# Modulation vectors of one layer computed beside another stage of a two-block model

## The chip, the cores and the metric

The kernel runs on 1 core of one Trainium2 chip. The metric is the device time of one execution in microseconds (us). PE is TensorE (the matrix engine), PEld its loads of stationary operands, DVE VectorE, ACT ScalarE, POOL GpSimd, SP SyncE, whose queue issues nearly all DMAs here.

## What is computed

The reference runs two blocks on 1024 latent rows of 1024 features, with context rows of 256 beside them. The first block has one layer: a mixer (half of the width a Hyena long convolution, half a bidirectional HGRN scan with four heads, which starts from the context's state) and a mixture of 16 experts. The second block has two layers of another mixer (Fourier, pooling, differential attention over context and latent rows). In both, vectors that depend on the conditioning alone scale and shift the rows:

```python
# first block
sh1, sc1, g1, sh2, sc2, g2 = jnp.split((s_lat @ ada_w[l] + ada_b[l])[:, None, :], 6, axis=-1)
h = modulate(rmsnorm(x, norm1_g[l]), sh1, sc1)
x = x + g1 * mix
h2 = modulate(rmsnorm(x, norm2_g[l]), sh2, sc2)
x = x + g2 * ec_moe(h2, ...)
...
# second block, layer l
shift, scale, gate = jnp.split(jax.nn.silu(c) @ w_mod + b_mod, 3, axis=-1)
shift_c, scale_c, gate_c = jnp.split(jax.nn.silu(c_ctx) @ w_mod + b_mod, 3, axis=-1)
hc = rms_norm(ctx, norm_g) * (1 + scale_c) + shift_c
```

The second block's `w_mod` is 1024 x 3072 for each layer. These products hang on no row of the latent or the context, so they can be made at any time before their first use.

## The kernel before

`run` (L1993) writes the whole program in stages. Each opens pools of tiles (a tag with a number of buffers, on the left or the right of the memory), and a tile of a tag waits until one of the tag's buffers is free. The program's order is not the engines' order: a planner (`schedule_with_timeline_sim`) fills each engine's queue at build time. Of the instructions that it holds ready it takes the one written first, so work written later fills the places that earlier work leaves. On the chip each queue then runs strictly in the order made.

The stages around the change, with the tiles by which the trace names them:

- *Projection stage.* Three streams are written interleaved by `side_by_side` (L1979): the Hyena filter and convolution (`filter_time`, `filter_spectra`, `hyena`; products into `pf`, their operands made in `y`, `t`, `fb`, `f`), the projections of the latent rows (`hy_proj`, `hg_proj`; weights `ar`, split into `ah` and `al`, products into `pp`, with the rows in `T`), and `mods_layer(0, ...)`, the modulation vectors of the second block's layer 0. `ctx_proj` of the stage ahead still runs at its beginning (`pp<-c,cr`).
- *The heads' stage.* `ctx_state` and four calls of `hgrn_head` (L944), two heads at a time in pools of their own (`hi`, `hw`, `hm`, `hT`, products into `ph`). A head runs seven levels: copies on ScalarE, products on TensorE, a masked copy (L985) and products over `hw` and `hT` on VectorE and GpSimd. A tail with more products follows. The heads read what the projections wrote, and their pools lie where the projections' tiles lay.
- *The context's work* of the second block is written behind the heads and fills in beside them: `mods_tail` (the rest of the first block's vectors: `g1`, `sh2`, `sc2`, `g2`), `ctx_first` (context rows, normed and modulated with layer 0's vectors), `ctx_side` (two column blocks, then `gate_steps`; products into `cp` and `cm`), and `mods_layer(1, ...)`.
- *Output product* `out_proj` (L1095; `pp<-wo,yt`), which reads `g1` and, in its router, `sh2` and `sc2`; then `topk`, then the experts (`moe`, products into `ea` and `ey`).

The change moves one call of `mods_layer` (L333). It runs `mod_rows` (L290) with three blocks of 1024 columns, each of eight k-steps:

```python
        for b0 in range(c0, c0 + ncols, 1024):
            ps = self.ps(pt)
            for k in range(8):
                if not pair:
                    r = self.t(raw[k % len(raw)])
                    self.dma(r, w[k * 128:k * 128 + 128, b0:b0 + 1024])
...
                for cb in range(2):
                    p0 = 64 * (k % 2) + 32 * cb
                    self.mm(ps[p0:p0 + 2], s[:, k, :], r[:, cb * 512:cb * 512 + 512], k < 2, k > 5)
```

One k-step is called a unit below: a load of 512 KB and, in the trace, four products with a stationary operand of two columns. A block ends with two bias loads, four additions on VectorE and two writes to DRAM. After the third block `rows_to_cols` (L315) reads the rows back as columns (two loads, one transpose, one copy), and two small operations make `A`. In `mods_layer(0, "mp", "u2", ("mr",), False)` the units pass through one buffer `mr`; in `mods_tail("cm", "cv", ("wr", "wr", "mr"), False)` through two buffers `wr` and one `mr`. The context's weights (`wcol`, then `wh` and `wl`) use `wr` too.

Of the kernel before, what the change touches and what calls it, by code (L numbers as in the profile page):

```python
# [1992 lines left out]
def run(K):  # L1993
    fst = ExitStack()
    with ExitStack() as e1:
        K.open(e1, "left", ar=3, ah=4, al=4)
        K.open_ps(e1, "left", pp=3, mp=1)
        K.open(e1, "left", u2=4, T=16)
        K.open_ps(fst, "right", pf=4)
        K.open(fst, "right", f4=7, fb=5)  # L2000
        with ExitStack() as e2:
            K.open(e2, "right", cr=6, x=4, c=2, mr=4)
            K.start()
        K.open(fst, "right", y=3, t=4, H=2, hs=3, dc=2, ri=7, ra=2, mr=1)
        K.load_dft()
        K.mods_first()
        side_by_side((30, 450, [(K.filter_time(), 2.4), (K.filter_spectra(), 2.1), (K.hyena(), 5)]),
                   (0, 64, [(K.hy_proj(), 1), (K.hg_proj(), 1)]),
                   (0, 4, [(K.mods_layer(0, "mp", "u2", ("mr",), False), 1)]))
    fst.close()  # L2010
    with ExitStack() as cx:
        with ExitStack() as e1:
            K.open_ps(e1, "left", ph0=3, ph1=3)
            K.open(e1, "left", hmk=1, hS=2)
            for p in "01":
                K.open(e1, "left", **{"hi" + p: 6, "hw" + p: 5, "h2" + p: 3, "hm" + p: 4, "hT1" + p: 2, "hT2" + p: 4})
            K.ctx_state()
            for h in range(4):
                K.hgrn_head(h)
            K.open(cx, "right", wr=2, wh=2, wl=2, cu=6, cv=2, Tc=4, lg=2)  # L2020
            K.pfx = "c"
            with ExitStack() as e2:
                K.open_ps(e2, "right", cp=1, cm=1)
                K.open(e2, "right", mr=1)
                for _ in K.mods_tail("cm", "cv", ("wr", "wr", "mr"), False):
                    pass
                K.ctx_first()
                K.ctx_side()
                for _ in K.mods_layer(1, "cm", "cv", ("wr", "wr", "mr"), False):
                    pass  # L2030
# [27 lines left out]
class Kern:  # L2058
# [9 lines left out]
    def start(self):  # L2068
        W = self.work
        W.pc, W.psm, W.pd, W.one = self.pc, self.psm, self.pd, self.one  # L2070
        run(W)
# [119 lines left out]
```

## Time and profile before

| | us |
|---|---|
| median of 3 runs | 3840.05 |
| lowest, highest | 3839.73, 3846.28 |
| the profiled execution | 3841.8 |
| its span, first to last instruction | 3839.7 |

By the page, TensorE is busy 92% of the span, VectorE 71%, ScalarE 58%, GpSimd 29%. Its table of 40 slices (96 us each) shows a DMA share of 0.9 and more only in the experts' part. The views used below are: the table of stretches (busy time of each engine in a stretch, count of instructions in brackets, the granted clock of TensorE as a share of full speed, the DMA engines' share and GB/s), groups of instructions (line, engine, operation, out<-in, shapes, count, then busy us and mean ns, then the idle time before them and what ended it), instructions by tile (least, median and most ns, first and last start), and the instructions in order of time.

### The profile page before, as it was taken

What the parts mean: (1) busy time and instruction counts of PE and PEld (TensorE: products, weight loads), DVE (VectorE), ACT (ScalarE), POOL (GpSimd) and SP (SyncE); (2) the same over time, 40 slices, a digit from 0 to 9 for tenths busy, and PEclk for the clock granted to TensorE, in tenths of its full rate; (3) what the DMA queues carried; (4) which work ended last, traced back from release to release, by engine and by line L of the source; (5) the groups of instructions that cost most, each with busy time, mean ns of one, the idle gap of its engine ahead of it and who ended that gap; (6) DMA issues with size and microseconds to landing.
All of it is one profiled execution on the core that took longest, in us unless ns stands there. A gap on an engine that the chain in (4) does not pass through costs nothing. (4 is left out here: it accounts for less than half of the span.)

```text
span 3839.7 us, 50939 instructions
## 1 busy us (share of the span) xinstructions
PE 3533.6 (92%) x17554; PEld 2841.9 (74%) x17554; DVE 2727.8 (71%) x4143; ACT 2219.1 (58%) x3568; POOL 1127.8 (29%) x702
## 2 busy tenths in 40 slices
PE   5998999968897799999999999979999899999989
PEld 2666878747867678787777777768777688877767
DVE  3488667777735789889889889866666744576672
ACT  4432322354525786787777777755576754456762
POOL 2355423364414214112112111001333610133361
PEclk9999999979998899999999999989999999999999
DMA  6765444464476699999999999952311144131133
GB/s 206 220 222 181 130 145 128 141 211 147 132 246 218 200 341 347 336 333 364 371 366 358 370 367 357 364 185 81 128 60 43 47 155 132 59 128 54 39 104 115
DMA packets 503019, 780.49 MB, mean 203 GB/s; under 512 B 35025, under 2 KB 238823, under 8 KB 502504
## 3 DMA queue, kind: packets, MB, share of 16 engines
q1 hardware_dynamic: 496136, 755.74, 57.8%
q0 software_dynamic: 5600, 20.43, 2.0%
q8 instruction: 138, 2.26, 0.2%
q10 hardware_dynamic: 1024, 1.06, 0.1%
q14 instruction: 121, 0.99, 0.1%
HBM read 669.00 MB, written 107.05 MB: 202 GB/s over the span
## 5 line engine op out<-in xcount | busy, mean ns | idle before, releaser
L171 DVE TENSOR_TENSOR el<-er,eh 128x1024 fp32r<-128x1024 f32 x763 | 950.7, 1296 | 107.9 <-ACT eh L168 105.8
L168 ACT ACTIVATE eh<-er 128x1024 fp32r<-128x1024 f32 x768 | 782.4, 1057 | 116.1 <-PE ea L190 83.5
L189 PE MATMUL ea<-el,xh 128*128 128x512 f32 x1024 | 413.9, 404 | 21.0 <-DVE el L171 18.1
L188 PE MATMUL ea<-eh,xh 128*128 128x512 f32 x1024 | 399.2, 393 | 2.4 <-ACT eh L168 2.2
L190 PE MATMUL ea<-eh,xh 128*128 128x512 f32 x1024 | 401.1, 392 | 0.0
L1265 POOL DMA_INDIRECT acc<-yo,idx x16 | 74.0, 4626 | 808.8 <-DVE yo L180 754.9
L1488 DVE TENSOR_SCALAR_CACHE_REDUCE E<-s,rq 128x512 f32<-128x512 f32 (+1 forms) x384 | 237.2, 656 | 80.8 <-PE s L193 70.0
L189 PEld LDWEIGHTS ea<-el,xh 128*128 128x128 f32 x1024 | 192.6, 188 | 94.1 <-DVE el L171 58.4
L165 ACT ACTIVATE E<-E,a 128x1280 f32<-128x1280 f32 x160 | 216.7, 1359 | 66.5 <-DVE a L1492 61.5
L193 PE MATMUL s<-KA,QA 128*128 128x512 f32 (+1 forms) x768 | 212.6, 398 | 32.1 <-DVE E L1488 31.1
L188 PEld LDWEIGHTS ea<-eh,xh 128*128 128x128 f32 x1024 | 192.5, 188 | 46.4 <-ACT eh L168 4.2
L190 PEld LDWEIGHTS ea<-eh,xh 128*128 128x128 f32 x1024 | 193.0, 189 | 34.3 <-POOL xh L171 0.3
L189 PE MATMUL ey<-el,hh 128*128 128x512 f32 x512 | 203.8, 398 | 6.2 <-DVE el L171 6.2
L188 PE MATMUL ey<-eh,hh 128*128 128x512 f32 x512 | 202.0, 399 | 2.1 <-ACT eh L168 2.1
L190 PE MATMUL ey<-eh,hh 128*128 128x512 f32 x512 | 200.3, 391 | 0.0
L171 POOL TENSOR_TENSOR wl<-wr,wh 128x1024 fp32r<-128x1024 f32 (+1 forms) x48 | 116.6, 2434 | 253.7 <-ACT wh L168 193.3
L193 PEld LDWEIGHTS s<-KA,QA 128*128 128x128 f32 x768 | 131.4, 199 | 78.8 <-DVE E L1488 60.3
L168 ACT ACTIVATE u<-pp 32x512 f32<-32x512 f32 (+2 forms) x212 | 124.4, 587 | 106.3 <-PE pp L190 85.6
L193 PE MATMUL po<-th,V 128*128 128x256 f32 x640 | 172.5, 395 | 13.7 <-ACT th L168 13.6
L188 PE MATMUL pp<-T,ah 128*128 128x512 f32 x448 | 183.0, 408 | 1.6 <-ACT ah L168 1.6
L190 PE MATMUL pp<-T,al 128*128 128x512 f32 x448 | 179.2, 400 | 0.4 <-POOL al L171 0.4
L189 PE MATMUL pp<-T,ah 128*128 128x512 f32 x448 | 178.7, 399 | 0.0
(516 smaller groups left out, 8944.2 us busy)
## 6 DMA issues: line engine op xcount, KB each, us to landing
er<-in_exp_w_dram SPq DMA_DIRECT2D x768, 512.0 KB
wr<-in_w_in_dram SPq DMA_DIRECT2D x60, 512.0 KB
ar<-in_w_in_dram SPq DMA_DIRECT2D x64, 256.0 KB
mr<-in_w_mod_dram SPq DMA_DIRECT2D x30, 512.0 KB
wr<-in_ada_w_dram SPq DMA_DIRECT2D x24, 512.0 KB
wr<-in_w_out_dram SPq DMA_DIRECT2D x24, 512.0 KB
Hd<-hs SPq DMA_DIRECT2D x72, 128.0 KB
H<-Hd SPq DMA_DIRECT2D x36, 256.0 KB
```

The costliest lines, as they stand in the source:

```text
L165: return self.nc.scalar.activation(out, in_, func, **kw)
L168: return self.nc.scalar.activation(out, in_, AF.Copy)
L171: return (eng or self.nc.vector).tensor_tensor(out, a, b, op=op)
L188: mm(out, lh, rh, start=first, stop=False)
L189: mm(out, lh, rl, start=False, stop=False)
L190: mm(out, ll, rh, start=False, stop=last)
L193: self.nc.tensor.matmul(out, l, r, start=first, stop=last)
L1265: nc.gpsimd.indirect_dma_start(out=self.acc, out_offset=x[0], in_=yo, in_offset=None, compute_op=ADD)
L1488: nc.vector.tensor_scalar(E[:, k0:k1], o, r, None, op0=MUL, op1=ALU.min, accum_out=mx[:, m, j:j + 1] if nc_ > 1 else mc)
```

## The change

The call `mods_layer(0, ...)` leaves the projection stage's interleaved streams, and with it goes the stage's buffer `mr`. Its 4 KB a partition go to the tags `y` (3 to 4 buffers of 2 KB) and `t` (4 to 5 buffers of 2 KB). The call is written instead at the head of the context's work, ahead of `mods_tail`, with the tags of `mods_tail`: product tile `cm`, small rows `cv`, loads through `wr`, `wr` and `mr` in turn. What it computes, and its number of instructions, stay.

```diff
-        K.open(fst, "right", y=3, t=4, H=2, hs=3, dc=2, ri=7, ra=2, mr=1)
+        K.open(fst, "right", y=4, t=5, H=2, hs=3, dc=2, ri=7, ra=2)
         K.load_dft()
         K.mods_first()
         side_by_side((30, 450, [(K.filter_time(), 2.4), (K.filter_spectra(), 2.1), (K.hyena(), 5)]),
-                   (0, 64, [(K.hy_proj(), 1), (K.hg_proj(), 1)]),
-                   (0, 4, [(K.mods_layer(0, "mp", "u2", ("mr",), False), 1)]))
+                   (0, 64, [(K.hy_proj(), 1), (K.hg_proj(), 1)]))
...
                 K.open_ps(e2, "right", cp=1, cm=1)
                 K.open(e2, "right", mr=1)
+                for _ in K.mods_layer(0, "cm", "cv", ("wr", "wr", "mr"), False):
+                    pass
                 for _ in K.mods_tail("cm", "cv", ("wr", "wr", "mr"), False):
                     pass
                 K.ctx_first()
```

## Rows read from the trace of the kernel before

**Rows 1.** the page, part 1: busy time, share and instructions of each engine

```profile
PE 3533.6 (92%) x17554; PEld 2841.9 (74%) x17554; DVE 2727.8 (71%) x4143; ACT 2219.1 (58%) x3568; POOL 1127.8 (29%) x702
```

**Rows 2.** stages; busy us (count) of PE, PEld, DVE, ACT, POOL; clock; DMA

```profile
112.00:775.00 663.00, 621.53 (x2878) 494.28 (x2877) 481.13 (x790) 203.70 (x434) 279.30 (x187) 0.97 0.52 165
775.00:1043.00 268.00, 214.84 (x1496) 175.25 (x1496) 204.86 (x351) 133.32 (x336) 148.45 (x117) 0.87 0.49 158
1043.00:1203.00 160.00, 148.47 (x762) 107.82 (x760) 57.38 (x98) 66.31 (x149) 31.02 (x22) 0.96 0.70 239
1290.00:2500.00 1210.00, 1178.38 (x5442) 946.90 (x5442) 1073.82 (x1018) 944.48 (x1130) 204.60 (x77) 1.00 1.00 352
```

**Rows 3.** first pair's levels, second pair's levels, heads' tail; columns as rows 2

```profile
835.00:885.00 50.00, 44.49 (x303) 32.63 (x302) 48.33 (x71) 35.45 (x104) 34.60 (x26) 0.91 0.48 169
943.00:1003.00 60.00, 47.26 (x351) 45.34 (x352) 59.49 (x80) 40.51 (x117) 45.88 (x34) 0.89 0.12 37
1003.00:1043.00 40.00, 39.01 (x334) 38.44 (x334) 19.47 (x42) 14.89 (x26) 12.67 (x7) 1.00 0.59 176
```

**Rows 4.** TensorE in order of time at 119 us: start, length, what

```profile
119.04 1.03 PE L193 MATMUL mp<-mr,silu 128*2 128x512 f32 x4
119.99 1.35 PE L193 MATMUL pp<-c,cr 128*128 128x256 f32 x5
```

**Rows 5.** groups on TensorE, 112 to 775 us: count, busy, mean ns, idle before

```profile
L193 PE MATMUL pf<-y,dc 128*128 128x256 f32 x448 | 122.4, 407 | 25.6 <-DVE y L171 13.3 <-POOL y L171 8.0 <-DVE y L180 2.8
...
L193 PE MATMUL mp<-mr,silu 128*2 128x512 f32 x92 | 27.7, 592 | 2.0 <-DMA mr<-in_w_mod_dram 1.9
```

**Rows 6.** tile mp, 105 to 775: ns least, median, most; first, last start

```profile
L193 PE MATMUL mp<-mr,silu x96: 591/592/592, 109.7 to 534.4; 128*2 128x512 f32 x96
L171 DVE TENSOR_TENSOR u<-u,mp x12: 669/680/690, 202.8 to 546.3; 2x512 f32<-2x512 f32 x12
```

**Rows 7.** TensorE in order of time, end of the projection stage

```profile
776.17 0.39 PE L189 MATMUL pp<-T,ah 128*128 128x512 f32 x1
776.40 0.39 PE L190 MATMUL pp<-T,al 128*128 128x512 f32 x1
```

**Rows 8.** tile pf (Hyena's products), 112 to 775 us; columns as rows 6

```profile
L193 PE MATMUL pf<-t,dc x256: 377/379/483, 456.7 to 739.2; 128*128 128x256 f32 x128
```

**Rows 9.** tile cm alone in two stretches: busy us (count) of PE, PEld, DVE

```profile
775.00:911.00 136.00, 31.36 (x128) 3.03 (x128) 10.87 (x16) 0.00 (x0) 0.83 0.61 205
1043.00:1203.00 160.00, 21.53 (x97) 2.35 (x97) 8.18 (x12) 0.20 (x1) 0.96 0.70 239
```

**Rows 10.** tile wr, 740 to 1043 us; columns as rows 6

```profile
L193 PE MATMUL cm<-wr,silu x96: 591/592/1061, 776.7 to 903.4; 128*2 128x512 f32 x96
L161 SPq DMA_DIRECT2D wr<-in_ada_w_dram x24: 327/352/909, 757.6 to 896.1; - x24
L161 SPq DMA_DIRECT2D wr<-in_w_in_dram x12: 373/384/910, 899.9 to 1038.6; - x12
```

**Rows 11.** VectorE's waits, 775 to 1043 us: total us, times, longest

```profile
DVE h L171 <- DMA hi<-df: 3.2, 1, 3.2
```

**Rows 12.** VectorE's products of the levels, 835 to 885 and 943 to 1003 us

```profile
L171 DVE TENSOR_TENSOR hw<-hw,hT 128x512 f32<-128x512 f32 x20 | 18.4, 923 | 0.0
L171 DVE TENSOR_TENSOR hw<-hw,hT 128x512 f32<-128x512 f32 x20 | 23.8, 1209 | 0.0
```

**Rows 13.** tile cp (the context's products) alone; columns as rows 9

```profile
895.00:1003.00 108.00, 20.26 (x126) 17.18 (x126) 0.00 (x0) 2.19 (x6) 0.87 0.30 93
1003.00:1043.00 40.00, 17.08 (x123) 15.43 (x124) 0.00 (x0) 1.85 (x5) 1.00 0.59 176
1043.00:1203.00 160.00, 7.20 (x57) 6.76 (x55) 0.00 (x0) 1.11 (x3) 0.96 0.70 239
```

**Rows 14.** tile wr, 1043 to 1145 us; columns as rows 6

```profile
L161 SPq DMA_DIRECT2D wr<-in_w_mod_dram x18: 327/332/403, 1046.0 to 1133.1; - x18
```

**Rows 15.** tile ea (the experts' first products); columns as rows 6

```profile
L188 PE MATMUL ea<-eh,xh x1024: 387/389/796, 1286.2 to 2494.0; 128*128 128x512 f32 x171
```

## Prediction

> **What bounds the kernel now.** I read the page's totals first: TensorE is busy 92% of the span [rows 1], but that is a mean over stages with different limits. The table of stages tells them apart [rows 2]. The change touches three of them. The projection stage (112 to 775 us) keeps TensorE busy 621.5 of 663 us, VectorE 481. The heads' stage (775 to 1043) keeps it busy 214.8 of 268 us. The stage of the output product (1043 to 1203) keeps it busy 148.5 of 160 us. Then a chain of top-k steps runs, and the experts move 352 GB/s with the DMA engines at a share of 1.00. The last two only begin later or earlier; they do not change length by this edit. So the time moves by what happens up to 1203 us, and there the first and third stage go by TensorE's queue.
>
> Next I asked which engine ends the heads' stage. While the first two heads run their seven levels, VectorE is busy 48.3 of 50 us; while the last two do, 59.5 of 60 us; in the tail after them TensorE is busy 39.0 of 40 us [rows 3]. So TensorE has room beside the levels only, and only a unit that runs there is hidden.
>
> **The change part by part.**
>
> *Taken out of the projection stage.* Layer 0's 24 units (one 512 KB load and four products each) are 96 products. A unit shows as 1.03 us, and the next product of the projection starts 0.95 us after its first one [rows 4]. 24 x 0.95 gives 22.8 us; as busy time 92 of them have 27.7 us, so 96 have 28.9 [rows 5]. The stage's own end is a projection product at 776.4 us [rows 7], while the last Hyena product starts at 739.2 [rows 8], so it is the projections' stream, which TensorE feeds, that releases the heads. I take -24 us. Bounds: -29 (all of the busy time), and -10, if much of these units now sits in time that TensorE would have idled (its idle time in the stage is 41.5 us [rows 2], spread over the stretch in which the units run). With them go 12 VectorE additions of 0.68 us [rows 6], 8.2 us on an engine busy 73% of the stage: I give them nothing of their own, since -24 already takes the stage as TensorE's. Their DMAs go too: 24 loads of some 0.35 us of queue time each [rows 10] and 14 small transfers.
>
> *The two buffers.* `y` and `t` gain one each. What they could shorten is TensorE's idle time before the transform products, 25.6 us, of which VectorE's and GpSimd's work on `y` ends 21.3 [rows 5]. That wait ends with the making of `y`, not with a buffer coming free, so I take 0 and keep -10 as the bound; a loss is excluded, since the queues only get one more place.
>
> *Put in front of the context's work.* The same 96 products go to the tile `cm`. There a stretch of 128 takes 31.4 us and one of 97 takes 21.5 us [rows 9], so 21 to 24 us of TensorE. Their cover is the 53 us that TensorE idles in the heads' stage [rows 2]; without the cover they would cost their 21 us in full. The loads decide how long they take. The second modulation (32 units, 24 loads into `wr` and 8 into `mr`) issues from 757.6 to 896.1 us, and the context's first weight follows at 899.9 [rows 10]: 138.5 / 32 = 4.3 us a unit, three buffers in turn, and the context's weights use the same `wr`. 56 units take 56 x 4.3 = 241 us. They start some 24 us sooner, at 734, and the context's first weight is issued at about 975 instead of 900. Against the heads, which I expect to end at 1043 - 24 - 5 = 1014, that leaves it 39 us instead of 143.
>
> *What waits behind them.* On SyncE's queue 24 loads and 14 small transfers now stand among the heads' loads. A load that waits for its buffer holds those behind it; what that has cost the heads so far is one wait of 3.2 us [rows 11]. I take 0, bounds 0 and +6 (twice). On VectorE 12 additions join the second modulation's 16 [rows 9]; some 8 of the 28 now fall beside the second pair's levels, where there were none: 8 x 0.68 = +5. The context's rows need layer 0's vectors and so wait until about 837 us (734 + 24 x 4.3); nothing but the context's own weights follows from them, and these wait for `wr` anyway: 0. The second modulation ends at about 975 instead of 903 us. Its gate row and its scale are first read by the output product and the router after 1014: 0, and if it ended later than that, each us would cost one.
>
> *What the heads gain.* The second pair's levels take 60 us against the first pair's 50 [rows 3]. The same 20 VectorE products over `hw` and `hT` take 1209 ns each there, against 923 [rows 12]; what is new beside them is the context's splitting of weights. After the change this is behind the levels. 10 us less, and the +5 above: -5, bounds -10 and 0. The Trainium skill, "SBUF — State Buffer" (SBUF: two separate sides), says that GpSimd and VectorE lock one pair of ports for a whole instruction and the loser blocks. By that rule the heads would gain the whole 10 us and the sum would be -16, 3824 us; the rows show the longer mean but not who held what.
>
> *What is displaced.* Before, TensorE did 126 of the context's products between 895 and 1003 us, beside the levels, 123 in the 40 us of the tail, and 57 after it, in 7.20 us [rows 13], which is 0.126 us each. With the context's first weight at 975 us, against levels that now end at about 974, the tail can take its 123 as before, and the 126 fall into the output product's stage: 126 x 0.126 = 16 us, and +18 with the context's small products in `cm`, an estimate from the same price. TensorE is busy 93% there, so this is paid. Bounds: +8 (half of the 126 find a place) and +34 (none of the 249 does: 31, and 3 for the small ones).
>
> **Sum**: -24 - 5 + 18 = -11 us. The profiled execution took 3841.8 us, of which 3839.7 are its span and 2.1 lie around it; the median of the three runs is 3840.05, 1.8 us lower. -11 gives 3830.8 for the one and **3829 us** for the other.
>
> **The rivals.**
>
> *The displaced work eats the gain.* The same mechanism with the terms nearer each other: -20 - 2 + 20 = -2, 3838 us. For it: work on TensorE is moved, not removed, and its idle time up to 1203 us (41, 53 and 12) only shrinks if the heads' stage takes more in than it gives away. Against it: units in `cm` cost less than those in `mp`, and the heads get shorter. Chance 0.27.
>
> *Slower: the modulations' loads outlast the heads.* All 56 units go through three buffers before the context's first weight. At 4.3 us a unit they end 39 us before the heads; from 5.0 us on (734 + 280 = 1014) no product of the context fits beside the heads, all 249 are paid in the full stage (+34), and the units that are left over stand between the output product's first rows. With -24, +34 and 4 for these that is +14, 3854 us. For it: twelve additions and 14 transfers more on queues that the heads use. Against it: the 24 units of layer 1 took 87 us by the stretch in which their loads issue, 3.6 us each [rows 14]. Chance 0.13.
>
> *Slower: the projection stage isn't TensorE's.* If the Hyena chain sets the stage, whose VectorE and GpSimd share tiles with it, the units were only filling, nothing is gained there, and the rest is -5 + 18 = +13, 3853 us. For it: TensorE's weight loads are busy 494 of 663 us only [rows 2], and 21 us of its idle time end with VectorE's or GpSimd's work on `y`. Against it: the stage's last projection products start 0.23 us apart, back to back [rows 7]. The Trainium skill, "Perfetto Trace Analysis" (Identifying the Most-Contended Engine), holds that the share of time in which matmuls run says little and asks for the weight loads' share. By that rule this rival is the forecast; the back-to-back products at the stage's end speak against it. Chance 0.09.
>
> *More than forecast.* The buffers let Hyena run ahead (-10), the stage gives back -29, the heads -10 and the displaced work costs +14: -35, 3805 us. Chance 0.12.
>
> **How the numbers follow.** The forecast (3822 to 3832) has 0.39, the rivals 0.27, 0.13, 0.09 and 0.12. About 0.2% (7.7 us) is what a measurement of this kernel tells from no change. Faster by more than that: the forecast and the large gain, 0.51. Within: 0.27. Slower: 0.22. The range leaves out half of the large gain and the ends of the slower cases: 3808 to 3853. The likeliest sign alone has 3808 to 3832.
>
> **What would show it.** The last product of the projections about 24 us earlier, with TensorE's idle time in that stage near 41 us; if that product comes less than 12 us earlier, the first step is wrong. The context's first `w_in` load near 975 us; later than 1014 us means the slower rival. The second pair's levels 50 to 56 us long, and the products over `hw` and `hT` back near 0.92 us. About 183 of the context's products after the heads' end, instead of 57. An output product that starts 29 us earlier and takes 178 us instead of 160. The prediction is wrong as a whole if the experts' first product, at 1286.2 us before [rows 15], isn't earlier by some 11 us, or if it is and the end does not follow.

## The result and the profile after

The changed kernel takes 3870.85 us (median of five runs, 3866.15 to 3875.72) against 3840.05 for the kernel before: a ratio of 1.0077, 95% interval 1.0064 to 1.009. It is some 30 us slower; 11 us faster was forecast. Its profiled span is 3869.2 us, before 3839.7.

I cut the span at the same five events in both traces: the last product of the projections, the last product of the heads (tile `ph`), the router's last rows (`lg<-pq`), and the first and last products of the experts (`ea`, `ey`). What follows, to the span's end, is the second block. A second profile of each kernel (the runs `before_again` and `after_again`, below) stands in brackets.

| stage, us | before | after | difference | forecast |
|---|---|---|---|---|
| projections end at | 776.8 (775.5) | 763.6 (767.8) | -13.2 | -24 |
| heads | 264.2 (264.3) | 259.4 (259.2) | -4.8 | -5 |
| output product, router | 161.7 (161.1) | 191.1 (191.0) | +29.4 | +18 |
| top-k | 83.5 (85.1) | 76.5 (76.1) | -7.0 | 0 |
| experts | 1220.8 (1219.9) | 1237.4 (1236.8) | +16.6 | 0 |
| second block | 1332.7 (1339.0) | 1341.2 (1338.5) | +8.5 | 0 |
| sum | 3839.7 | 3869.2 | +29.5 | -11 |

So three things went wrong: half of the gain in the projection stage did not come, the output product's stage lost over half as much again as forecast, and behind the router, where nothing was expected, another 18 us are missing.

The page's totals of the changed kernel (part 1, as [rows 1]) say nothing of this: the work is the same.

```profile
PE 3531.8 (91%) x17554; PEld 2855.2 (74%) x17554; DVE 2738.1 (71%) x4143; ACT 2222.0 (57%) x3570; POOL 1120.9 (29%) x702
```

The table of stretches does, with the columns of [rows 2]: projections, heads, output product, experts.

```profile
112.00:763.00 651.00, 597.05 (x2786) 498.09 (x2787) 472.18 (x776) 201.96 (x430) 274.21 (x188) 0.96 0.48 149
763.00:1023.00 260.00, 206.66 (x1363) 151.14 (x1362) 206.69 (x355) 122.19 (x316) 121.44 (x103) 0.89 0.56 188
1023.00:1214.00 191.00, 178.23 (x987) 137.74 (x985) 66.20 (x105) 77.65 (x168) 51.67 (x34) 0.94 0.67 222
1290.00:2528.00 1238.00, 1195.11 (x5487) 960.85 (x5487) 1089.94 (x1042) 953.83 (x1149) 212.92 (x82) 0.99 0.98 345
```

Against [rows 2], TensorE's busy time in the projection stage falls by 24.5 us (621.5 to 597.1), but its idle time rises from 41.5 to 54.0 us. In the output product's stage its busy time rises from 148.5 to 178.2 us, and its idle time stays at 12.8 (11.5 before). In the experts' part the DMA share falls from 1.00 to 0.98, and VectorE is busy 11 us longer (1078.7 us before and 1089.9 after, each between its own first and last product of the experts; the stretches shown cut it differently).

The first pair's levels, the second pair's, and the heads' tail, as [rows 3], at the same distance from the levels' own products:

```profile
815.00:866.00 51.00, 43.36 (x292) 31.41 (x292) 50.75 (x73) 32.81 (x99) 32.83 (x25) 0.94 0.47 162
918.00:978.00 60.00, 47.85 (x322) 36.34 (x321) 59.32 (x89) 36.50 (x108) 39.13 (x28) 0.91 0.41 139
978.00:1023.00 45.00, 42.10 (x293) 35.41 (x293) 18.54 (x41) 13.19 (x25) 7.45 (x5) 0.92 0.64 194
```

VectorE is as full beside the second pair's levels as before, but the length of that stretch is my choice. The levels' own ends show in their masked copies, before and after:

```profile
L985 DVE COPY_PREDICATED hw<-hmk,ph x28: 702/727/747, 942.7 to 1002.5; 128x512 f32<-128x512 uint8 x28
```

```profile
L985 DVE COPY_PREDICATED hw<-hmk,ph x28: 704/727/751, 919.6 to 975.6; 128x512 f32<-128x512 uint8 x28
```

From the first to the start of the last they take 59.8 us before and 56.0 after. From there to the heads' end it is 38.5 us before and 47.4 after: the tail grows by 9 us. TensorE is busy 42.1 of the 45 us shown, at a granted clock of 0.92 (1.00 in [rows 3]), although the context does little there; the last 32 products of the modulations now run in it. The context's products (tile `cp` alone, as [rows 13]), in the changed kernel before and after the heads' end, and in the kernel before from the heads' end on:

```profile
963.00:1023.00 60.00, 6.11 (x36) 4.99 (x37) 0.00 (x0) 0.75 (x2) 0.91 0.48 146
1023.00:1214.00 191.00, 35.13 (x270) 33.84 (x269) 0.00 (x0) 4.44 (x12) 0.94 0.67 222
```

```profile
1041.00:1202.80 161.80, 9.20 (x72) 8.76 (x72) 0.00 (x0) 1.11 (x3) 0.96 0.71 240
```

270 of them now fall into the output product's stage, for 35.1 us, instead of 72 for 9.2 us ([rows 13] has 57, since it starts 2 us behind the heads' end). The loads through `wr` (as [rows 10], with layer 0's now ahead) show when its weights come: the first is issued at 990.2 us, not 899.9.

```profile
L161 SPq DMA_DIRECT2D wr<-in_ada_w_dram x24: 327/332/1132, 865.6 to 985.3; - x24
L161 SPq DMA_DIRECT2D wr<-in_w_mod_dram x18: 327/342/1160, 743.3 to 859.6; - x18
L161 SPq DMA_DIRECT2D wr<-in_w_in_dram x12: 372/384/522, 990.2 to 1100.7; - x12
```

Every third load of the modulations goes through `mr`. There the chain of loads starts earlier than in `wr`, at 739.6 us in the kernel before and at 725.5 in the changed one:

```profile
L161 SPq DMA_DIRECT2D mr<-in_ada_w_dram x8: 328/332/417, 739.6 to 889.4; - x8
```

```profile
L161 SPq DMA_DIRECT2D mr<-in_w_mod_dram x12: 328/380/964, 725.5 to 1181.6; - x12
```

The end of the projection stage, as [rows 7], and the Hyena group that holds most of TensorE's idle time there, as in [rows 5]:

```profile
763.03 0.39 PE L189 MATMUL pp<-T,ah 128*128 128x512 f32 x1
763.26 0.39 PE L190 MATMUL pp<-T,al 128*128 128x512 f32 x1
```

```profile
L193 PE MATMUL pf<-y,dc 128*128 128x256 f32 x448 | 121.2, 413 | 38.7 <-DVE y L171 29.6 <-ACT hs L168 3.0 <-ACT f L165 2.9
```

The stage still ends with projection products back to back, and yet TensorE waits longer ahead of the transform products: 38.7 us, of which VectorE's work on `y` ends 29.6, against 25.6 and 13.3 in [rows 5]. The experts' first product, as [rows 15], comes 4.4 us later than before:

```profile
L188 PE MATMUL ea<-eh,xh x1024: 387/389/628, 1290.6 to 2515.0; 128*128 128x512 f32 x171
```

### The profile page after: what moved, and what is told of

It is laid out like the page before. It is cut to its first block, busy times and chain, and to the rows that moved or that the text cites. A ratio compares the mean times of both kernels' runs of the same rounds, so it can differ in the third digit from the quotient of the medians.

```text
span 3869.2 us, 50934 instructions
## 1 busy us (share of the span) xinstructions
PE 3531.8 (91%) x17554; PEld 2855.2 (74%) x17554; DVE 2738.1 (71%) x4143; ACT 2222.0 (57%) x3570; POOL 1120.9 (29%) x702
```

## The experiments

Ratios are to the kernel before on the same chip, with 95% intervals. Where a kernel's stage ends are given they are from its profile, cut as above.

### What the units cost in the projection stage

**before_no_l0** leaves layer 0's products out of the kernel before.

```diff
-        yield from self.mod_rows(I["w_mod_2"][l], ...)
+        if l == 0:
+            self.dma(self.m2[l], I["b_mod_2"][l].partition_broadcast(2))
+        else:
+            yield from self.mod_rows(I["w_mod_2"][l], ...)
```

> The kernel before with layer 0's products left out altogether (the vectors are then the bias rows alone, so the output is not the reference's); buffers, streams and the rest stay. It prices the removal by itself. Theory 1 (the units had filled time in which TensorE would have waited for VectorE's work on the Hyena tiles): the projections end some 13 us earlier (764 us instead of 777), TensorE's idle time between 110 us and that end rises by some 12 us, and the time is near 3827 us. Theory 2 (the stage is TensorE's, as forecast; the two added buffers spoil it in the changed kernel): the projections end 24 us earlier, near 753 us, idle time unchanged, 3816 us.

3842.67 us, ratio 0.9999 (0.999 to 1.0008). The projections end at 760.7 us, 16 earlier. The stretch of that stage and the same Hyena group:

```profile
112.00:760.00 648.00, 592.61 (x2787) 495.63 (x2788) 483.61 (x778) 201.07 (x432) 276.07 (x188) 0.96 0.47 150
```

```profile
L193 PE MATMUL pf<-y,dc 128*128 128x256 f32 x448 | 122.6, 408 | 37.3 <-DVE y L171 25.0 <-DVE y L180 8.5 <-POOL y L171 2.9
```

TensorE's busy time is 28.9 us shorter than in [rows 2], the units' own, and its idle time 55.4 us, 13.9 longer: about half of the units had filled time in which it would have waited for VectorE's `y` (25.0 us here, 13.3 in [rows 5]). In the stage that is what theory 1 said. Its time, 3827, did not come.

**before_no_l0_again** and **before_again** are second profiles of that kernel and of the kernel before, since a gain of 16 us in a stage and none in the time do not go together.

> The kernel before without layer 0's products (bias rows alone) once more, for a second profile. If the stage lengths belong to its queues: projections end again within 4 us of 760.7, the experts again within 4 us of 2495, and the second block again takes 1340 us and more, against 1333 and 1339 in the two profiles of before. If it is chance: the projections end anywhere from 760 to 772 us, or the second block is near 1335 us and the execution near 3830.

> The kernel before once more, for a second profile. Its second block took 1332.7 us in the first one, those of eight variants 1334 to 1346. If that is the order of the queues, it is 1333 us again within 3; if it is chance from one execution to the next, it may be anywhere up to 1345, and a gain ahead of the experts' end then shows in the time only as a mean.

The stage repeats: projections end at 761.5 us, experts at 2492.1 (2495.0 in the first profile); in the two of before the experts end at 2507.0 and 2506.0. So about 13 us are gained up to there. The second block took 1343.2 and 1337.7 us without the units, 1332.7 and 1339.0 with them: it differs by 6 us between two executions of one kernel, and the two means differ by 4.6. The two profiled executions, 3839.9 and 3831.7 us, also both lie under that kernel's median of 3842.7. What becomes of the 13 us in the mean time is not settled by two profiles.

**l1_in_proj** adds to that stage: layer 1's 24 units go there as well, from the output product's stage.

```diff
-                   (0, 4, [(K.mods_layer(0, "mp", "u2", ("mr",), False), 1)]))
+                   (0, 8, [(K.mods_layer(0, "mp", "u2", ("mr",), False), 1), (K.mods_layer(1, "mp", "u2", ("mr",), False), 1)]))
...
-                for _ in K.mods_layer(1, "cm", "cv", ("wr", "wr", "mr"), False):
-                    pass
```

> The kernel before with layer 1's 24 units moved from behind the context's work (they run in the output product's stage, where TensorE is busy 93%) into the projection stage behind layer 0's. Theory 1 (units in the projection stage cost nothing): the output product's stage loses their 20 us, what follows begins 20 us earlier, and the time is 3820 to 3828 us. Rival (the projection stage is TensorE's): 23 us later at the end of the projections, the sum within 5 us of before. Second rival (TensorE does not set the output stage's length either): the stage stays over 155 us.

3844.38 us, ratio 1.0008 (0.9999 to 1.0017). Projection stage and output product's stage:

```profile
112.00:804.00 692.00, 646.26 (x2975) 494.80 (x2976) 485.69 (x803) 203.26 (x433) 276.77 (x187) 0.97 0.55 176
1068.00:1209.00 141.00, 129.41 (x685) 110.89 (x684) 50.68 (x83) 66.27 (x150) 33.20 (x21) 0.93 0.53 185
```

The projections end 28 us later (804.9), so here 24 units cost all of their busy time; TensorE's idle time, 45.7 us, no longer shrinks. The output product's stage falls by 21 us to 140.9. The rival holds: the units only change places.

**tail_in_proj** puts the rest of the first block's vectors (32 units) there.

```diff
-                   (0, 4, [(K.mods_layer(0, ...), 1)]))
+                   (0, 8, [(K.mods_layer(0, ...), 1), (K.mods_tail("mp", "u2", ("mr",), False), 1)]))
...
-                for _ in K.mods_tail("cm", "cv", ("wr", "wr", "mr"), False):
-                    pass
```

> The opposite of the change: the kernel before with the rest of the first block's vectors (32 units) also in the projection stage, through its one buffer mr and its tile mp, and none of them beside the heads. Leaving layer 0's 24 units out of that stage had changed the time by 0. Theory 1 (a unit costs nothing in the projection stage, and costs beside the heads by holding the context's work back): the projections end at most 10 us later, the context's first weight is issued before 830 us, layer 1's units move beside the heads, the output product's stage falls from 162 us by 15 to 25, and the time is 3820 to 3835 us. Rival (the projection stage is TensorE's, as forecast): its end moves 30 us back, 32 units at 0.95 us, and the time is 3840 to 3850 us.

3871.35 us, ratio 1.0082 (1.0068 to 1.0096). Projections, heads, output product:

```profile
112.00:810.00 698.00, 655.69 (x3013) 494.31 (x3014) 495.26 (x807) 207.08 (x438) 282.28 (x190) 0.97 0.57 182
810.00:1089.00 279.00, 216.61 (x1513) 185.19 (x1512) 223.57 (x348) 134.89 (x340) 145.47 (x118) 0.87 0.44 142
1089.00:1226.00 137.00, 121.82 (x609) 102.33 (x608) 42.92 (x82) 61.86 (x142) 23.26 (x17) 0.90 0.48 167
```

34 us more in the projections for 32 units, 14 more beside the heads (VectorE 223 us against 205 in [rows 2]), 24 less in the output product. Theory 1 falls, and the rival was too mild.

The three runs together: TensorE's idle time in the projection stage is 55 us without units, 41.5 with 24, 45.7 with 48, 42.3 with 56. The first 24 filled 14 us of it, and those added behind them filled nothing more. A unit is worth 0.6 us where it is taken away and 1.1 us or more where it is added. The added units also run later in the stage (behind 534 us, where layer 0's end), and TensorE was fuller there already (96% of 534 to 775 us in the kernel before, 93% ahead of it); direction and place are not told apart.

### What the two buffers do

**old_buffers** is the changed kernel with the old counts; **y4_t4** takes back only the fifth `t`; **after_again** is the changed kernel once more.

```diff
-        K.open(fst, "right", y=4, t=5, H=2, hs=3, dc=2, ri=7, ra=2)
+        K.open(fst, "right", y=3, t=4, H=2, hs=3, dc=2, ri=7, ra=2)
```

> The changed kernel with three buffers of y and four of t, as before; only the call is moved. Theory 1 (a wait for y ends when y is made, not when a buffer comes free): projections end within 3 us of the changed kernel's 763.6 us, and the time is the same, 3871 us within 6. Rival (the buffers let the filter's work run ahead of the projections and spoil the stage): projections end near 753 us, and the time is near 3860. Rival (they help): the projections end 5 to 10 us later, 3878.

> The changed kernel with four buffers of y and four of t, to be held against after_again on the same chip. With three and four (the run old_buffers) the projections ended at 758.4 us, with four and five at 763.6. Theory 1 (the extra buffers let the filter's work run ahead of the projections on TensorE's queue, the fourth y above all): the projections end near 764 us and the time is that of after_again within 3 us. Rival (the fifth t does it): they end near 758 us, and the time is 4 to 6 us under after_again.

> The changed kernel once more, unchanged: a second profile of it, and its time beside y4_t4 on one chip. If the stage lengths are the queues' own, each stage up to the experts' end is within 2 us of the first profile (763.6, 259.4, 191.1, 76.5 and 1237.4 us) and the second block again near 1341 us; if they are chance, they differ by as much as those of different kernels do, 5 us and more.

old_buffers 3865.24 us, ratio 1.0066 (1.0053 to 1.0079); y4_t4 3867.09, 1.0063 (1.005 to 1.0076); after_again 3868.81, 1.0072 (1.0059 to 1.0085). The projections end at 758.4, 762.5 and 767.8 us (763.6 in the first profile of the changed kernel). In the stage the changed kernel is 5 to 9 us longer with the buffers; taking back the fifth `t` alone takes back 1 to 5 of them. The time cannot tell the three apart.

**after_no_l0** and **after_no_l0_again** are the changed kernel without layer 0's products, by the diff of before_no_l0. Against before_no_l0 the buffers differ, and the place of layer 0's few small operations.

> The changed kernel with layer 0's products left out (bias rows alone, output not the reference's): buffers as changed, nothing added in front of the context's work. Against the changed kernel it prices the addition, against the run before_no_l0 the two buffers. Theory 1 (the added units push the context's products out of the heads' stage, and that goes on into the top-k and the experts): projections end near 764 us as in the changed kernel, the context's first weight is issued near 890 us instead of 990, the output product's stage is back near 162 us from 191, and the time near 3827 us, 44 us under the changed kernel. Theory 2 (the loss is the new order of the later stages, not the units): the time stays within 10 us of the changed kernel's 3871.

> The changed kernel without layer 0's products once more, for a second profile. By the queues: projections end again near 771 us, second block near 1338. By chance: the projections end nearer the 758 to 768 us of the other kernels without layer 0's units in this stage.

3845.98 us, ratio 1.0012 (1.0004 to 1.0021). Projections and output product:

```profile
112.00:771.00 659.00, 598.50 (x2788) 499.13 (x2788) 473.57 (x776) 201.79 (x430) 280.29 (x187) 0.95 0.46 148
1041.00:1202.00 161.00, 149.28 (x783) 108.78 (x782) 59.22 (x97) 66.95 (x151) 32.81 (x21) 0.97 0.72 240
```

The projections end at 771.3 and, the second time, at 770.3 us, against 760.7 and 761.5 with the old buffers: 10 us that belong to the kernel's queues, not to chance. TensorE idles 60.5 us instead of 55.4 and is busy 6 us longer, at a granted clock of 0.95 against 0.96. In both pairs the stage is longer with more buffers. Other versions with the new counts end it at 760 to 769 us, though, and before_written_first (below), with the old counts and an edit far behind this stage, ends it at 770.1 instead of 776.8. So the size of it hangs on the rest of the plan too, and how much the buffers do by themselves is not shown; which order of the queues does it was not tried.

The output product's stage is back at 161 us, as theory 1 said; its time, 3827, did not come. What the units cost in their new place follows from the experts' ends: 2528.0 and 2531.0 us with them, 2505.9 and 2506.1 without, 22 to 25 us; by the ratios 0.6%, 23 to 25 us.

### Why the context is late

**own** keeps the modulations' loads and the context's weights in buffers of their own: two `wr` for the one, `mr` for the other.

```diff
-                for _ in K.mods_layer(0, "cm", "cv", ("wr", "wr", "mr"), False):
+                for _ in K.mods_layer(0, "cm", "cv", ("wr",), False):
...
+                K.rtag = "mr"
                 K.ctx_side()
+                K.rtag = None
...
-        t = self.t(w + "r", [128, shape[0] * shape[1]])
+        t = self.t(self.rtag or w + "r", [128, shape[0] * shape[1]])
```

> The changed kernel with the raw weights apart: the modulations' loads go through the two buffers wr alone, the context's through the one buffer mr, so that neither waits for a buffer of the other. Theory 1 (the context's weights come late only because they queue for wr behind 56 units): the context's first weight is issued near 880 us instead of 990, TensorE's context work in the output product's stage falls from 35 us to some 12, that stage from 191 us to some 168, and the time to about 3846 us. Rival (TensorE has no room in the heads' stage for both, or SyncE's queue holds the loads back in any case): the stage stays near 190 us, with the modulations' products in the place of the context's, and the time within 8 us of 3871.

3880.55 us, ratio 1.0105 (1.009 to 1.0119): slower still. The modulations, now with two buffers instead of three, end at 1015 us instead of 990. The context's first weight is loaded at 723 us, and its first products follow at 921 instead of 996:

```profile
L189 PE MATMUL cp<-Tc,wh x24: 277/283/561, 921.3 to 1054.1; 128*128 128x256 f32 x24
```

And yet its products in the output stage take 39.6 us:

```profile
1024.00:1221.00 197.00, 39.58 (x280) 36.98 (x280) 0.00 (x0) 4.91 (x13) 0.93 0.64 214
```

So the weights' queue for `wr` does hold the context's first products (996 us, 6 behind the first weight, in the changed kernel), but freeing it is not enough: as the whole explanation it falls. The products into `cm` show what holds the context next: the modulations' last, and the context's first small product (a transpose).

```profile
L194 PE MATMUL cm<-wr,silu x224: 589/592/1061, 760.3 to 1014.3; 128*2 128x512 f32 x112
...
L197 PE MATMUL cm<-ident,cu x2: 264/264/264, 1026.1 to 1026.6; 4*128 4x4 f32 x2
```

The context's small products need the one tile `cm`, and the modulations hold it, block after block, until 1014. In the changed kernel the seven blocks hold it from 763.6 to 990.4 us. Between two of them it stands still; here the last of these gaps, on TensorE and then on VectorE:

```profile
954.25 1.03 PE L193 MATMUL cm<-wr,silu 128*2 128x512 f32 x4
...
975.90 1.04 PE L193 MATMUL cm<-wr,silu 128*2 128x512 f32 x8
```

```profile
959.82 0.66 DVE L171 TENSOR_TENSOR cv<-cv,cm 2x512 f32<-2x512 f32 x1
...
966.06 1.39 DVE L171 TENSOR_TENSOR cv<-cv,cm 2x512 f32<-2x512 f32 x2
...
972.05 0.69 DVE L171 TENSOR_TENSOR cv<-cv,cm 2x512 f32<-2x512 f32 x1
```

The block's last four products begin at 954.25 us, the next block's first at 975.90; between them lie the four additions, spread over 13 us on a VectorE that is full with the heads. Six such gaps, from 8 to 21 us, sum to 84 of the 227 us. The Trainium skill, "Perfetto Trace Analysis" (Matmuls), asks that independent groups of products rotate through different banks of the product memory, so that one group is read out while the next runs; these gaps agree. A second `cm` was not tried: the stage has its tiles given out, three and three to the heads, one to `cp` and one to `cm`.

**ctx_ahead** writes the context's work between the two modulations.

```diff
-                for _ in K.mods_tail("cm", "cv", ("wr", "wr", "mr"), False):
-                    pass
                 K.ctx_first()
                 K.ctx_side()
+                for _ in K.mods_tail("cm", "cv", ("wr", "wr", "mr"), False):
+                    pass
```

> The changed kernel with the context's work (its rows and its two column blocks and gates) written between layer 0's vectors and the rest of the first block's vectors. In the trace of the run own the context's small products waited for the one product tile cm, which the modulations fill block by block, until the last modulation ended. Theory 1 (the chain of 56 modulation units through the one tile cm holds the context back): the first context product comes near 880 us instead of 996, some 100 and more of its big products go back beside the heads, and the context takes under 20 us of TensorE in the output product's stage instead of 35. The 32 units that now end late are read by the output product, so the sum can be anything from 3845 to 3880 us. Rival (the heads leave TensorE no room): the context's share of the output stage stays over 30 us.

3895.15 us, ratio 1.014 (1.0125 to 1.0156). The context's big products begin at 896 us instead of 996, and 72 of them are left for the output stage, 10.9 us, instead of 270:

```profile
L188 PE MATMUL cp<-Tc,wh x96: 278/283/510, 896.2 to 1037.4; 128*128 128x256 f32 x96
```

That is the count of the kernel before, from the heads' end on. So the units written ahead of it did hold the context back, and the heads leave TensorE room for it. This run frees the weights' buffers and `cm` together; own freed the buffers alone (and left the modulations one less) and won nothing. The two together point to `cm`; no run frees `cm` alone. But the other vectors are late now, and that costs more: the output product's stage takes 222.7 us, and TensorE idles 35 us of it.

```profile
1022.00:1245.00 223.00, 187.69 (x913) 114.84 (x913) 70.64 (x114) 67.30 (x152) 33.69 (x21) 0.89 0.74 253
```

**after_written_first** writes the two modulations ahead of the heads, so that their additions go first on VectorE.

```diff
-            for h in range(4):
-                K.hgrn_head(h)
...
                 for _ in K.mods_tail("cm", "cv", ("wr", "wr", "mr"), False):
                     pass
+                K.pfx = ""
+                for h in range(4):
+                    K.hgrn_head(h)
+                K.pfx = "c"
```

> The changed kernel with layer 0's vectors and the rest of the first block's vectors written ahead of the heads instead of behind them; the context's rows and columns stay behind the heads. Theory 1 (between blocks the one tile cm is held 8 to 21 us by additions that wait on VectorE's queue behind the heads): the gaps between blocks in cm shrink below 5 us, the last of the 56 units ends near 910 to 930 us instead of 990, the context takes under 20 us of TensorE in the output product's stage instead of 35, that stage falls from 191 to 165 to 175 us, and the time is 3840 to 3855 us if the heads lose less than 5 us. Rival (the loads' pace sets the units, 4.6 us each): the last unit still ends after 970 us and the time stays within 8 us of 3869. Second rival (the additions now hold up the heads, whose stage VectorE sets): the heads' stage grows by 10 us and more, and nothing is won.

3851.9 us, ratio 1.0024 (1.0015 to 1.0033): 17 to 19 us under the changed kernel, inside theory 1's range. But the way there is only partly the one I named: the last unit starts at 970.3 us, not 910 to 930, and the gaps still sum to 65 us of the 84, so the order of the additions behind the heads makes only a part of them. The heads' stage grows by 3 us (262.4).

```profile
L193 PE MATMUL cm<-wr,silu x168: 591/592/1061, 762.3 to 970.3; 128*2 128x512 f32 x168
```

```profile
1024.00:1202.00 178.00, 167.44 (x937) 128.53 (x935) 60.40 (x97) 74.63 (x164) 49.48 (x29) 0.98 0.69 232
```

20 us earlier for the context took 13 us off the output product's stage (191.0 to 178.0) and 5.5 us off what follows the router.

**before_written_first** does the same to the kernel before, where four blocks stand in `cm`.

> The kernel before with the rest of the first block's vectors (32 units) written ahead of the heads instead of behind them. Theory 1: the four blocks in cm end near 860 us instead of 904, the context follows 40 us earlier, layer 1's units begin beside the heads, and the output product's stage falls from 162 us by some 10 to 20: 3822 to 3832 us, faster than both kernels. Rival (the heads lose on VectorE and in their loads what the context wins): within 6 us of before.

3852.93 us, ratio 1.003 (1.0019 to 1.0041). The four blocks' last product ends at 897 us (904 before), but only because the projections end 7 us earlier; from there it is 127 us in both. The heads take 270.0 us instead of 264.2, the output product's stage stays at 161.0. Nothing is won, and the rival was too mild. No version that computes everything beats the kernel before.

### What sets the output product's stage, and what follows it

**after_no_l1** leaves layer 1's products out of the changed kernel, by the diff of before_no_l0 with `l == 1`.

> The changed kernel with layer 1's products left out (bias rows alone, so the output is not the reference's). Theory 1 (the output product's stage is TensorE's): that stage falls from 191 us by the 20 us that layer 1's units hold TensorE in it, to about 171; the context, still late by the rest, keeps the experts' part 4 to 8 us long, and the time is 3840 to 3848 us. Rival (the late context hangs on its own chain of weights, splits and product tile, not on TensorE): the stage falls by less than 10 us, or the experts' part stays at 1313 us behind the router's last rows, and the time is 3852 us or more.

3826.56 us, ratio 0.9964 (0.9952 to 0.9976), 42 us under the changed kernel and more than either theory gave. The output product's stage:

```profile
1031.00:1187.00 156.00, 145.74 (x841) 127.21 (x840) 52.62 (x90) 74.47 (x164) 49.64 (x29) 0.97 0.56 190
```

It falls from 191.1 to 155.5 us, by TensorE's 32.5 us there (178.2 to 145.7): 20 of layer 1, 7 because the context got more of its products done beside the heads (224 left instead of 270), and the other 6 because the stage's own products, the same in number, took less time, at a granted clock of 0.97 against 0.94. TensorE idles 10 us of it, and 8 to 15 in every version of this stage but ctx_ahead: 162 us with 150 busy before, 191 with 178 in the changed kernel, 178 with 167 in after_written_first, 156 with 146 here, 141 with 129 in l1_in_proj. That stage is TensorE's. The experts' part is back to 1220.6 us.

**l1_late** moves layer 1's units of the kernel before behind the top-k steps.

```diff
                 K.topk()
                 K.pfx = "c"
+                for _ in K.mods_layer(1, "cm", "cv", ("wr",), False):
+                    pass
                 K.ctx_heads("tw")
```

> The kernel before with layer 1's 24 units written behind the top-k steps instead of ahead of the output product, through the two buffers wr; layer 0 stays in the projection stage. In the runs so far, what followed the router's last rows took the same time to the experts' end (1301 to 1304 us in five kernels), whatever ran ahead. Theory 1 (the output stage is TensorE's, 150 of 162 us, and the top-k stage has room, TensorE busy 53 of 83 us): the router's last rows come 15 to 20 us earlier, the experts' part follows, and the time is 3820 to 3828 us. Rival (the units and their loads fall among the experts' first loads, or hold the context's heads back): what is won before the router's end is lost behind it, and the time is within 5 us of before, or over it.

3870.18 us, ratio 1.0073 (1.006 to 1.0086). Output product, then top-k:

```profile
1039.00:1180.00 141.00, 132.60 (x726) 107.63 (x725) 49.62 (x87) 64.64 (x148) 28.25 (x19) 0.98 0.60 207
1180.00:1290.00 110.00, 67.46 (x394) 49.48 (x394) 66.22 (x99) 35.36 (x73) 45.19 (x29) 0.73 0.74 222
```

The router's last rows come 22 us earlier, as theory 1 said, but the top-k stage takes 109.5 us instead of 83.5 and the experts 1237.0. So what is won ahead of the router is lost behind it, as the rival said, and 20 us more: the experts end at 2526.7 us, 2507.0 in the kernel before. From the router's last rows to the experts' end it is 1346 us. In ten profiles (two each of before, before_no_l0 and after_no_l0, and tail_in_proj, l1_in_proj, before_written_first, after_no_l1) that distance is 1301 to 1305 us, whatever ran ahead. In the changed kernel it is 1313.9 and 1312.9, in own 1316, in after_written_first 1308.

What the ten share is not how much of the context was done by the heads' end (after_no_l1 leaves 224 products to the output stage, as after_written_first does), but where its attention starts. Its first tile `cE` comes 9.6 to 11.0 us ahead of the experts' first product in the ten, 7.0 us ahead in after_written_first and ctx_ahead (1308 and 1310 us), and 0.2 us behind it in both profiles of the changed kernel, own, old_buffers, y4_t4 (1311 to 1316) and l1_late.

Half of the 16.6 us by which the experts' part grows is lost in the first expert (8 us), all of it by the sixth. TensorE's waits in the first expert of the changed kernel show two for the context's attention, which has none there in the kernel before (us in total, times, longest):

```profile
PE cp L193 <- POOL cQA L176: 5.2, 1, 5.2
PE cp L193 <- DVE cE L1488: 2.7, 1, 2.7
```

More of it shows in the group of the experts' products that need VectorE's half of a split weight (`el`), in the first 564 us of the experts' part before and 570 us after; the last entries are TensorE's idle time ahead of them and what ended it:

```profile
L189 PE MATMUL ea<-el,xh 128*128 128x512 f32 x448 | 180.5, 403 | 6.6 <-DVE el L171 6.1
```

```profile
L189 PE MATMUL ea<-el,xh 128*128 128x512 f32 x434 | 176.9, 408 | 12.9 <-DVE el L171 12.7
```

The wait for `el` doubles from 6.1 to 12.7 us. There the context's attention runs beside the experts, and more of it now: VectorE makes all 16 of its `cE` tiles in that stretch instead of 12. From the sixth expert on the distance between the two kernels no longer changes.

## Why the prediction was wrong, step by step

**Taken out of the projection stage, -24.** Half right. The stage fell by 13.2 us; without the new buffers it falls by 15 to 18 (before_no_l0, old_buffers). The step that failed is the choice between its bounds: I gave the whole 0.95 us of each unit because the stage ends with projection products back to back. They are back to back in every version, which shows only what TensorE does last. What decides is how its idle time changes, and there the lower bound (-10, "time that TensorE would have idled") was the nearer one: 14 of 29 us came back as idle time (before_no_l0), nearly all of it ended by VectorE's `y`. The Trainium skill's rule that I set beside it, "Perfetto Trace Analysis" (Identifying the Most-Contended Engine), pointed, as I read it, to the opposite extreme, a stage that isn't TensorE's and no gain (its weight loads are busy 498 of 651 us now); removal lies between the two, and adding units behind layer 0's cost their time in full.

**The two buffers, 0.** "A loss is excluded, since the queues only get one more place" was wrong. The stage is 5 to 11 us longer with them in two pairs of kernels, one that differs in them alone and one that nearly does. That a buffer more changes what the planner can place earlier, and so the order on every queue, is my reading; the runs show the length, not the cause.

**What the heads gain, -5.** It came, -4.8, by luck. The products over `hw` and `hT` are back at 901 ns beside the second pair (forecast 0.92 us):

```profile
L171 DVE TENSOR_TENSOR hw<-hw,hT 128x512 f32<-128x512 f32 x20 | 17.8, 901 | 0.1
```

But the levels are only 4 us shorter (56.0 instead of 59.8), with 89 VectorE instructions beside them instead of 80, and the tail behind them, which I took as unchanged, is 9 us longer. What makes up for it, some 10 us, lies ahead of the second pair's levels, where I had no term. The Trainium skill, "SBUF — State Buffer" (SBUF: two separate sides), would have had the heads gain all 10 us. GpSimd is busy 39.1 us there instead of 45.9 [rows 3] and VectorE's products are a quarter shorter, which agrees with that rule, as does ctx_ahead, where the context's splitting is back beside the levels and the same products take 1255 ns; no run here shows who held the ports.

**What is displaced, +18.** The step that failed is the count: +29.4 us, a miss as large as the first one. Its price was right (0.13 us a product; 270 took 35.1 us). The count was wrong, 183 expected (198 counted from the heads' end), 270 found. "The tail can take its 123 as before" assumed that the context would run at full pace as soon as its weights were there. It began at 996 us, 27 before the heads' end, with small products that wait on each other, in a tail that TensorE fills with the heads' own work and the last units; only 36 got done between 963 and 1023 us. My upper bound, +34, said just this, and I took the value between. The loads' pace was misread: [rows 10] holds the loads through `wr` alone, and the first through `mr` went out at 739.6 us. That makes 156.5 / 32 = 4.9 us a unit instead of 4.3, and 56 units from 716 us end at 990, which is when the first weight was issued (990.2; the loads began at 725.5 us and took 4.7 each, so that the agreement is partly luck). But the weights are only one holder: own and ctx_ahead point to the chain through `cm` as the second, and under what waits behind the units the prediction doesn't name it.

**Behind the router, 0.** "They do not change length by this edit" failed too: +9.6 us for top-k and experts together. Work on the context that is late goes on being late, through the top-k steps (7 us shorter, with less of it in them) into the first five experts (16 us longer), where TensorE waits for the context's attention and its VectorE work delays the split weights.

**The second block, 0.** +8.5 us in the first pair of profiles, but +4.0 between the means of two each, with 6 us between two executions of the same kernel. What of it belongs to the queues stays open.

**The rivals.** The one that came nearest in its consequence is "the modulations' loads outlast the heads": most of the context's products paid in the output stage. Its condition did not come about: 4.7 us a unit, first weight 33 us ahead of the heads' end. I had tied the consequence to a threshold that it does not need. Even so its time, 3854 us, is 17 us short: it has the projections at -24 and nothing behind the router.

**The sum with the measured terms**: -13.2 - 4.8 + 29.4 + 9.6 + 8.5 = +29.5, the distance between the two spans. By the ratios of whole executions, taking the units out of the projection stage is worth nothing (0.9999), the new buffers cost 0.1% (1.0012), and the units in their new place 0.6% (1.0072 and 1.0077).

## What to carry to other kernels

Work taken out of an engine's queue is worth what the queue's idle time does not take back, and back-to-back work at a stage's end does not tell that. In this stage a removal was worth half and an addition all of its busy time, so keep both bounds until a run says which holds. Before moving filler ahead of other filler, follow every single-buffered tile that both use, the product tile as well as the load buffers, and ask how long the last of the chain leaves the work behind it before the cover ends. Late filler can be paid again in each later stage that it slips into.

## What the runs showed that was not expected

Stage lengths ahead of the experts' end repeat between two profiles of one kernel within 1 to 4 us (projections 760.7 and 761.5, 771.3 and 770.3, 763.6 and 767.8), so 10 us there can be read from one profile. The second block varies more: 1332.7 and 1339.0 us in the kernel before, 1343.2 and 1337.7 in before_no_l0. With the DMA engines at a share of 0.99 between the experts' first and last product, the experts end 1301 to 1305 us behind the router's last rows in ten profiles, so a gain ahead of the router reaches the experts' end in full if the context's attention starts on time.
